# A hybrid decoder layer: gate/up products summed in PSUM, paced weight sums, a new order of the down products

## The chip, the core and the metric

The kernel runs on one core of a Trainium2 chip. The metric is the device time of one execution in microseconds (us). The kernel is compared with an earlier version of itself. An execution is also recorded by the hardware profiler; its times count from the start of the recorded span. TensorE is called PE in the rows, VectorE DVE, ScalarE ACT, GpSimd POOL, and SP is the queue that issues the transfers.

## What is computed

One decoder layer in fp32 with 1024 tokens of width 1024: attention in two kinds, a normalisation, then a feed-forward part (FFN) of width 2816 and a second normalisation. The change is in the FFN:

```
y  = concat(FoX out, GLA out) @ W_o
x  = layer_norm(alpha * x + (1 + gate_m) * y, ln1_g, ln1_b)
u2 = x * (1 + scale_f) + shift_f
h  = silu(u2 @ w_gate) * (u2 @ w_up)          # (1024, 2816)
y2 = h @ w_down                               # (1024, 1024)
x  = layer_norm(alpha * x + (1 + gate_f) * y2, ln2_g, ln2_b)
```

## The kernel before

All operands of matmuls are split in a high part (`hi`, made by an ACT cast, L87) and a low part (`lo`, the rest, made by a DVE subtraction, L88); a product is hi x hi + hi x lo + lo x hi, so three matmuls for each pair of tiles. `split` is that pair of operations.

Gate/up: the 2816 columns are taken in 22 blocks of 128 (index f). In each block, gate and up together form a matrix that is cut in 2 x 2, the input is cut in 2 x 2 as well (A11, A12, A21, A22), and the eight products of the quarters are replaced by seven, P1 to P7, of sums of quarters. The sums of the input (S1 to S4) are made once (`second_operands`), those of the weights (T1 to T4) once a block (`sum_weights`, four DVE operations L982 to L985, and splits). Each product is 12 matmuls of 128 x 512 into a PSUM bank (`product`, L996). P1 and P2 need only A11 and A12, so the first three blocks' P1 and P2 run first, while ACT and DVE make the rest. In `group_parts` P1 and P2 are added up in a half of the two-bank tile `c11`; P3 goes into `y_` on top of P5, P4 (`x_`) on top of P7, P6 has a bank `z_`; DVE and ACT then add the parts: five additions a block on DVE (L1071, L1079, L1081, L1082, L1086) and a multiplication with the gate (L1087).

The down product uses seven products as well. Its sums of h (`h_sums`, stored to DRAM in `a_d`) and of the rows of w_down (`w_sums`, L1034 to L1040, loaded, four DVE operations, stored to `t_d`) are made during gate/up, `w_sums` for two blocks at a time (NI = 11 of them). In `ffn_down` a down product (924 matmuls in all, L1167) is written as `product(banks, columns of a_d, rows of w, new)`; (k, c) names the part k of a_d and the half c of the tokens. It runs over 6 groups: each loads two tiles (`ar`, `raw`), splits them, and multiplies into four banks, `sa` or `sb`. Between products the rows of the residual come in (`rows_in`, L1108 to L1110: a load of z_d, a POOL multiplication with l1g, a POOL addition of l1b), results are added to them (`add_rows`, L1180 on POOL, L1181 on DVE), and `out_norm` (L1231 to L1241) writes the final rows.

The order of the instructions on each engine is set by a scheduler that works from its own estimate of durations, with the program's order as priority; `after(key)` adds the condition that what follows is placed behind a recorded instruction. Pools of fixed slots decide when a tile can be written again: `slot(i)` waits until the last reader of slot i is through.

## Time and profile before

| | us |
|---|---|
| median of 3 runs | 1314.95 |
| lowest, highest | 1314.1, 1317.26 |
| the profiled execution | 1316.09 |
| its span | 1314.4 |
| TensorE busy in the span | 1240.2 |
| DVE busy | 826.6 |
| ACT busy | 507.6 |
| POOL busy | 275.9 |

Busy times overlap, and the share of an engine over the whole span is a mean of stages with different limits. The FFN takes the span from about 609 us on. The page's chain of work that ended last runs for 66% of the span over TensorE, for 13% over transfers and for 10% over DVE. A matmul's record is longer than its distance to the next (0.39 against 0.23 us), since matmuls are pipelined; time is therefore told from start to start.

### The profile page before, as it was taken

Reading aid. Unit: us, or ns where it says so; the run is one execution under the profiler, and the core shown is the slowest. Engines: PE = TensorE matmul, PEld = TensorE weight load, DVE = VectorE, ACT = ScalarE, POOL = GpSimd, SP = SyncE. Lnnn points to the kernel's source line nnn. Section 1 sums busy time; section 2 is a strip of 40 time slices with the busy share of each in tenths; the row PEclk is TensorE's granted clock in tenths of the full one; section 3 lists DMA queues with packets and bytes.
Section 4 is the critical chain, followed back from the end, with each engine's and each line's share of the span. In section 5 each row is a group of like instructions: output and inputs, shape, how many; then the busy total and the mean of one; then the engine's idle time right before and its main releaser. Section 6 shows DMA issues by size and latency. Waiting matters only on the chain.

```text
span 1314.4 us, 16515 instructions
## 1 busy us (share of the span) xinstructions
PE 1240.2 (94%) x6209; PEld 996.8 (76%) x6209; DVE 826.6 (63%) x1207; ACT 507.6 (39%) x858; POOL 275.9 (21%) x264
## 2 busy tenths in 40 slices
PE   6999999999999999999899989999999969999994
PEld 4889987899877656667577768888888847888873
DVE  7656537732465455556987776675675577654768
ACT  3422354523354466565532222332233313443331
POOL 3500023220245355231000000000000067200225
PEclk9999999999999999999999999999999979999988
DMA  9865621112125115144387774332322485666543
GB/s 298 257 224 174 214 65 33 25 25 65 49 97 145 66 33 146 65 144 144 108 259 265 233 253 147 120 113 96 120 70 83 153 325 163 192 208 190 165 142 128
DMA packets 137297, 190.67 MB, mean 145 GB/s; under 512 B 7953, under 2 KB 87931, under 8 KB 137217
## 3 DMA queue, kind: packets, MB, share of 16 engines
q1 hardware_dynamic: 137216, 189.61, 45.2%
q8 instruction: 49, 0.80, 0.3%
...
HBM read 140.94 MB, written 44.32 MB: 141 GB/s over the span
## 4 chain that ended last, share of the span: by engine, by line
PE 66%; DMA 13%; DVE 10%; issue 3%; ACT 3%; POOL 3%; SPq 1%; POOLq 0%; DVEq 0%; ACTq 0%
PE dn L1167 12%; PE gu L996 7%; PE gy L996 6%; PE gx L996 6%; PE pv L791 4%; DMA t_d<-wd 3%; DMA wc<-in_w_c_dram 3%; PE gz L996 3%; DMA wd<-in_w_down_dram 3%; PE tr L781 3%; PE acc L330 3%; PE acc L332 3%; PE acc L331 3%; PE acc L100 2%; PE acc L99 2%
## 5 line engine op out<-in xcount | busy, mean ns | idle before, releaser
L88 DVE TENSOR_TENSOR lo<-raw,hi 128x1024 fp32r<-128x1024 f32 (+1 forms) x112 | 146.4, 1307 | 170.6 <-ACT hi L87 170.5
L87 ACT CAST hi<-raw 128x1024 fp32r<-128x1024 f32 (+1 forms) x112 | 114.8, 1026 | 134.4 <-PE gu L996 46.1
L1167 PE MATMUL dn<-hi,al 128*128 128x512 f32 x280 | 111.1, 402 | 13.6 <-DVE al L88 13.6
L1167 PE MATMUL dn<-lo,ah 128*128 128x512 f32 x280 | 112.4, 401 | 3.5 <-DVE lo L88 3.5
L1109 POOL TENSOR_TENSOR r<-r,l1g 128x1024 f32<-128x1024 f32 x8 | 23.0, 2896 | 437.9 <-PE gu L996 435.5
L1167 PE MATMUL dn<-hi,ah 128*128 128x512 f32 x280 | 110.9, 401 | 1.1 <-ACT ah L87 0.8
L330 PE MATMUL acc<-hi,uh 128*128 128x264 f32 (+1 forms) x384 | 108.8, 284 | 0.9 <-ACT m L531 0.8
L332 PE MATMUL acc<-hi,ul 128*128 128x264 f32 (+1 forms) x384 | 108.7, 284 | 0.0
L331 PE MATMUL acc<-lo,uh 128*128 128x264 f32 (+1 forms) x384 | 108.7, 283 | 0.0
L88 DVE TENSOR_TENSOR al<-ar,ah 128x1024 fp32r<-128x1024 f32 (+1 forms) x38 | 58.2, 1539 | 50.6 <-ACT ah L87 50.5
L1167 PEld LDWEIGHTS dn<-hi,al 128*128 128x128 f32 x280 | 54.0, 193 | 27.7 <-DVE al L88 14.9
L330 PEld LDWEIGHTS acc<-hi,uh 128*128 128x128 f32 x384 | 72.8, 190 | 2.3 <-ACT m L531 1.0
L331 PEld LDWEIGHTS acc<-lo,uh 128*128 128x128 f32 x384 | 72.8, 190 | 0.6 <-issue 0.2
L332 PEld LDWEIGHTS acc<-hi,ul 128*128 128x128 f32 x384 | 72.7, 189 | 0.4 <-issue 0.2
L756 DVE CUSTOM_DVE_ANT_0 pr<-sc,smask 128x128 f32<-128x128 f32 (+7 forms) x64 | 47.6, 754 | 38.1 <-PE sc L752 23.2
L87 ACT CAST ah<-ar 128x1024 fp32r<-128x1024 f32 (+1 forms) x38 | 37.3, 984 | 88.2 <-PE dn L1167 83.4
L1167 PEld LDWEIGHTS dn<-lo,ah 128*128 128x128 f32 x280 | 54.0, 193 | 16.6 <-DVE lo L88 4.3
L996 PE MATMUL gu<-a1h,lo 128*128 128x512 f32 x160 | 63.9, 399 | 2.3 <-DVE lo L88 2.3
L996 PE MATMUL gy<-s,b 128*128 128x512 f32 x264 | 64.5, 391 | 1.1 <-DVE hf L1071 0.6
L1167 PEld LDWEIGHTS dn<-hi,ah 128*128 128x128 f32 x280 | 53.8, 192 | 14.3 <-ACT ah L87 1.2
L786 ACT COPY pt<-tr 128x512 f32<-128x512 f32 x80 | 45.7, 583 | 46.3 <-PE tr L781 39.1
L996 PE MATMUL gu<-a1l,hi 128*128 128x512 f32 x160 | 63.3, 396 | 0.0
...
## 6 DMA issues: line engine op xcount, KB each, us to landing
ar<-a_d SPq DMA_DIRECT2D x35, 512.0 KB, 4.1
wc<-in_w_c_dram SPq DMA_DIRECT2D x32, 512.0 KB, 4.5
raw<-in_w_gate_dram SPq DMA_DIRECT2D x25, 512.0 KB, 5.4
wd<-in_w_down_dram SPq DMA_DIRECT2D x22, 512.0 KB, 4.4
t_d<-wd SPq DMA_DIRECT2D x22, 512.0 KB, 5.2
a_d<-hf SPq DMA_DIRECT2D x22, 512.0 KB, 5.0
u<-in_w_up_dram SPq DMA_DIRECT2D x21, 512.0 KB, 3.9
raw<-t_d SPq DMA_DIRECT2D x20, 512.0 KB
```

The lines of the kernel that those rows point to most:

```text
L87: nc.scalar.copy(dst_hi, src)
L88: return nc.vector.tensor_tensor(dst_lo, src, dst_hi.bitcast(F32), op=ALU.subtract).ins
L99: nc.tensor.matmul(ps, lh, rh, start=start, stop=False)
L330: nc.tensor.matmul(ps, uh[k][:, ts], wh[:, k % 4, :], start=k == 0, stop=False)
L331: nc.tensor.matmul(ps, uh[k][:, ts], wl[:, k % 4, :], start=False, stop=False)
L332: nc.tensor.matmul(ps, ul[k][:, ts], wh[:, k % 4, :], start=False, stop=k == NK - 1)
L756: nc.vector.tensor_tensor_reduce(t[:, 0:nk], sc[:, 0:nk], smask[:, S - nk : S], op0=ALU.add, op1=ALU.min, scale=-1.0, scalar=3e38, accum_o ...
L781: nc.tensor.transpose(tr[:, a * 256 + j * P : a * 256 + (j + 1) * P], ps_[2 * j + par][:, (2 * kk + a) * P : (2 * kk + a + 1) * P], ident,)
L786: nc.scalar.copy(pt[:, par, :], tr)
L791: nc.tensor.matmul(pv[64 * par : 64 * par + 64, 0:256], fv_t(kb)[:, 64 * h : 64 * h + 64], pt[:, par, a * 256 : (a + 1) * 256], start=kb == 0,
L996: nc.tensor.matmul(ps, x, y, start=start and j == 0 and i == 0, stop=j == NJ - 1 and i == 2, skip_group_check=not start,)
L1167: nc.tensor.matmul(ps, x[:, a, qs], y[:, a, :], start=start and a == 0 and i == 0, stop=stop and a == n - 1 and i == 2, skip_group_check=n ...
```

## The change

1. `group_parts`: P6 and P7 and P4 are added in PSUM to P1 in bank `a`, P3 to P5 in `c`; P2 has a bank `b`. DVE adds three times a block (L1077, L1090, L1092), ACT copies three times and applies silu twice. The order is P1 P2 P6 P5 P7 P3 P4; in block 0 P5 comes before P6.
2. `second_operands`: the sums of S3 come first, its splits last but one. P1 and P2 of the first three blocks are written block by block.
3. `w_sums` is called at the blocks WS = 3, 4, 6, 8, 10, 12, 13, 15, 17, 19, 21, each behind that block's load of up weights; `h_sums` of a pair is called in the next pair's first block.
4. `ffn_down`: `sa` is four single banks, `sb` halves of two-bank tiles, the product (3, 0) comes before (2, 1), and the vectors l1g, l1b, gf, l2g, l2b and the residual's rows are loaded between the groups (`between`), behind the loads of the group before. The multiplication with gf goes from POOL to DVE.

```diff
-        stage("S3", 0, a11, a11, a21, ALU.subtract, "t")
-        stage("S1", 1, a21, a21, a22, ALU.add, "sS3")
-        stage("A22", 4, a22, None, None, None, "sS1")
-        stage("S2", 2, a22, a22, a11, ALU.subtract, "lo")
-        stage("S4", 3, a12, a12, a22, ALU.subtract, "sS2")
+        with after("t"):
+            sums(a11, a11, a21, ALU.subtract)
+        stage("S1", 1, a21, "sum", a21, a22, ALU.add)
+        stage("A22", 4, a22, "sum")
+        stage("S2", 2, a22, "lo", a22, a11, ALU.subtract)
+        stage("S3", 0, a11, "sum")
+        stage("S4", 3, a12, "sum", a12, a22, ALU.subtract)
...
-        nc.sync.dma_start(u, w_up[:, f * P : (f + 1) * P].rearrange("(k p) n -> p k n", p=P))
+        last["u"] = nc.sync.dma_start(u, w_up[:, f * P : (f + 1) * P].rearrange("(k p) n -> p k n", p=P)).ins
...
         def p1():
-            product(c11, w["B11"], opnd["A11"], True)
+            if f == 2:
+                st_["a"] = bank("b2", "ga")
+            else:
+                st_["w"] = wide(f"w{par}", "ga")
+                st_["a"] = st_["w"][:, 0:512]
+            product(st_["a"], w["B11"], opnd["A11"], True)
 
...
+            if f < 2:
+                st_["b"] = st_["w"][:, 512:1024]
             else:
...
+                st_["b"] = bank("b3" if f < 4 else f"b{2 + par}", "gb")
+            product(st_["b"], w["B21"], opnd["A12"], True)
...
+        def p6():
+            h = st_["h"] = h_tile(f)
+            nc.scalar.copy(h[:, 0, :], st_["a"])
+            if f == 0:
+                g0 = cp.tile([P, 512], F32, tag="m1", name="g0")
+            else:
+                st_["g"] = slot(HG[par], (2, 512), name="sg")
+                g0 = st_["g"][:, 0, :]
+            st_["g0"] = g0
+            nc.vector.tensor_tensor(g0, st_["b"], h[:, 0, :], op=ALU.add)
+            product(st_["a"], w["T2"], opnd["S2"], False)
+            nc.scalar.activation(g0, g0, AF.Silu)
+            nc.scalar.copy(h[:, 0, :], st_["a"])
+
+        def p5():
+            st_["c"] = bank(f"b{par}", "gc")
+            product(st_["c"], w["T1"], opnd["S1"], True)
+
+        def p73():
+            a, c_, h = st_["a"], st_["c"], st_["h"]
+            nc.scalar.copy(h[:, 1, :], c_)
+            product(a, w["T3"], opnd["S3"], False)
+            nc.vector.tensor_tensor(h[:, 1, :], a, h[:, 1, :], op=ALU.add)
+            product(c_, w["B22"], opnd["S4"], False)
+            nc.vector.tensor_tensor(h[:, 0, :], c_, h[:, 0, :], op=ALU.add)
+
+        def p4():
             h = st_["h"]
...
+            last["p4"] = product(st_["a"], w["T4"], opnd["A22"], False)
+            if f == 0:
+                st_["g"] = slot(HG[par], (2, 512), name="sg")
+            g = st_["g"]
+            nc.scalar.activation(g[:, 1, :], st_["a"], AF.Silu)
...
+            else:
+                nc.vector.tensor_tensor(h, g, h, op=ALU.mult)
...
-        wides = [wide(f"w{1 - i}", "dn") for i in range(2)]
-        sa = [wides[q // 2][:, (q % 2) * 512 : (q % 2 + 1) * 512] for q in range(4)]
-        sb = [bank(f"b{q}", "dn") for q in range(4)]
+        sa = [bank(f"b{q}", "dn") for q in range(4)]
+        wides = [wide(f"w{i}", "dn") for i in range(2)]
+        sb = [wides[q % 2][:, (q // 2) * 512 : (q // 2 + 1) * 512] for q in range(4)]
...
+        def product(banks, asrc, bsrc, new, between={}):
             for m in range(NG):
+                if m in between:
+                    with after("ld"):
+                        between[m]()
                 g = group(m, asrc, bsrc)
...
-            nc.gpsimd.tensor_tensor(t, t, gf[:, hs], op=ALU.mult)
+            gf = cv["gf"]
+            nc.vector.tensor_tensor(t, t, gf[:, hs], op=ALU.mult)
...
-        ra = rows_in(0)
-        product(sa, a_cols(0, 0), w_rows(0, 0), True)
...
+        def gains():
+            cv["l1g"], cv["l1b"] = bcast(14, ln1_g, "l1g"), bcast(15, ln1_b, "l1b")
+            for n in ("l1g", "l1b"):
+                nc.scalar.mul(cv[n], cv[n], ALPHA)
...
+        product(sa, a_cols(0, 0), w_rows(0, 0), True, {2: gains, 3: rows_of(0, 0), 4: rows_of(0, 1), 5: rows_of(0, 2)})
...
+        product(sb, a_cols(1, 0), w_rows(1, 0), True, {1: rows_of(0, 3), 2: load("gf", 22, grow_d[3, :])})
...
+        product(
+            sa, a_cols(2, 0), t_rows(1, 1), False, {3: load("l2g", 24, ln2_g), 5: load("l2b", 26, ln2_b)}
...
+        product(sb, a_cols(0, 1), t_rows(0, 0), True, {m: rows_of(1, m - 1) for m in range(1, 5)})
...
-        rb = rows_in(1)
+        product(sb, a_cols(3, 0), w_rows(1, 1), False)
+        for q in range(4):
+            nc.vector.tensor_tensor(c2[q], sb[q], c2[q], op=ALU.add)
+            add_rows(ra, bsa, q, 1, c2[q])
+            out_norm(0, q, ra[q], bsa[q], l2g, l2b)
         product(sa, a_cols(2, 1), t_rows(0, 1), False)
         bsb = [new_bs() for q in range(4)]
         for q in range(4):
             nc.vector.tensor_tensor(c5[q], sa[q], c5[q], op=ALU.add)
             add_rows(rb, bsb, q, 1, c5[q])
-        product(sb, a_cols(3, 0), w_rows(1, 1), False)
-        for q in range(4):
-            nc.vector.tensor_tensor(c2[q], sb[q], c2[q], op=ALU.add)
-            add_rows(ra, bsa, q, 1, c2[q])
-            out_norm(0, q, ra[q], bsa[q])
...
-        gs[0][0]()
-        gs[1][0]()
-        gs[0][1]()
-        gs[1][1]()
-        gs[2][0]()
-        gs[2][1]()
+        for f in range(3):
+            gs[f][0]()
+            gs[f][1]()
+    WS = [3 + i * 18 // 10 for i in range(NI)]
...
-        p754()
-        p63()
+        if f == 0:
+            p5()
+            p6()
+        else:
+            p6()
+            p5()
         if f >= 2 and f % 2 == 0:
-            w_sums(f // 2 - 1)
-    w_sums(NI - 1)
...
+            h_sums(f // 2 - 1)
+        p73()
+        p4()
+        if f in WS:
+            with after("u"):
+                w_sums(WS.index(f))
+    h_sums(NI - 1)
```

**SP at the second operands.** The rows run from the last store of z_d (its readers are the residual's rows later on) to the first loads for `w_sums`. Before, with `raw` the gate and `u` the up weights of blocks 1 and 2:

```order
L883 DMA z_d<-r_5338 128x1024 [waits Activation_49]
L960 DMA raw_5910<-in_w_gate_dram 128x8x128 [waits DMAHW7_49]
L960 DMA raw_6012<-in_w_gate_dram 128x8x128 [waits DMAHW1_49]
L965 DMA u_6014<-in_w_up_dram 128x8x128 [waits DMAHW0_49,PE_49]
L965 DMA u_5912<-in_w_up_dram 128x8x128 [waits PE_49]
L1034 DMA wd_6105<-in_w_down_dram 128x1024 [waits DMAHW2_49,DVE_49]
L1034 DMA wd_6106<-in_w_down_dram 128x1024 [waits DMAHW3_49,DVE_49]
```

Now:

```order
L883 DMA z_d<-r_5338 128x1024 [waits Activation_49]
L969 DMA u_6000<-in_w_up_dram 128x8x128 [waits PE_49]
L969 DMA u_5909<-in_w_up_dram 128x8x128 [waits DMAHW7_49,PE_49]
L964 DMA raw_5907<-in_w_gate_dram 128x8x128 [waits DMAHW0_49]
L964 DMA raw_5998<-in_w_gate_dram 128x8x128 [waits DMAHW1_49]
L969 DMA u_6118<-in_w_up_dram 128x8x128 [waits DMAHW7_49,DMAHW2_49,DVE_49]
L1039 DMA wd_6220<-in_w_down_dram 128x1024 [waits DMAHW3_49]
L1039 DMA wd_6221<-in_w_down_dram 128x1024 [waits DMAHW4_49,DVE_49]
```

The two up loads, which wait for PE, have moved ahead of the two gate loads.

**DVE at the same place.** `af` and `x` are quarters of the input, L943 (now L942) a sum for S1 to S4, L88 the low part of a split, L982 (now L986) the first sum of a block's weights. Before:

```order
L943 TENSOR_TENSOR af_5340<-af_5340,x_934_5629 128x512 [waits Activation_49]
L943 TENSOR_TENSOR af_5357<-af_5357,x_935_5630 128x512 [waits Activation_49]
L88 TENSOR_TENSOR s_946_5682<-af_5340,s_946_5682 128x512 [waits Activation_49]
L88 TENSOR_TENSOR s_947_5686<-af_5357,s_947_5686 128x512 [waits Activation_49]
L943 TENSOR_TENSOR af_5374<-af_5374,x_936_5631 128x512 [waits Activation_49]
L943 TENSOR_TENSOR af_5391<-af_5391,raw_5632 128x512 [waits Activation_49]
L943 TENSOR_TENSOR x_934_5629<-x_934_5629 128x512
L943 TENSOR_TENSOR x_935_5630<-x_935_5630 128x512
```

Now:

```order
L1077 TENSOR_TENSOR g_5848<-ga_5757,hf_5846 128x512 [waits Activation_49]
L942 TENSOR_TENSOR af_5340<-af_5340,x_934_5629 128x512 [waits Activation_49]
L942 TENSOR_TENSOR af_5357<-af_5357,x_935_5630 128x512 [waits Activation_49]
L942 TENSOR_TENSOR af_5374<-af_5374,x_936_5631 128x512 [waits Activation_49]
L986 TENSOR_TENSOR raw_5907<-u_5909,raw_5907 128x512 [waits DMAHW7_49,DMAHW0_49]
L942 TENSOR_TENSOR af_5391<-af_5391,raw_5632 128x512 [waits Activation_49]
L942 TENSOR_TENSOR x_934_5629<-x_934_5629 128x512 [waits DVE_49]
L942 TENSOR_TENSOR x_935_5630<-x_935_5630 128x512 [waits DVE_49]
L942 TENSOR_TENSOR x_936_5631<-x_936_5631 128x512 [waits DVE_49]
L987 TENSOR_TENSOR u_5909<-u_5909 128x512 [waits DVE_49,PE_49]
```

A weight sum of block 1 that waits for two transfers has moved from behind the splits of S1 to the fifth place, and an addition of block 0's P1 and P2 (L1077) stands ahead.

**PE at the first down product.** `gy` and `gc` are gate/up banks of the last block, `dn` the banks of the down product. Before:

```order
L996 MATMUL gy_8563<-s_962_5742,b_1302_8520 128x512 [waits DVE_49]
L996 MATMUL gy_8563<-s_962_5742,b_1302_8520 128x512 x2
L996 MATMUL gy_8563<-s_963_5746,b_1302_8520 128x512 x3
L996 MATMUL gy_8563<-s_964_5750,b_1302_8520 128x512 x3
L996 MATMUL gy_8563<-s_965_5754,b_1302_8520 128x512 x3
L1167 MATMUL dn_8655<-hi_8683,ah_8681 128x512 [waits Activation_49]
L1167 MATMUL dn_8655<-lo_8684,ah_8681 128x512
L1167 MATMUL dn_8656<-hi_8683,ah_8681 128x512
L1167 MATMUL dn_8656<-lo_8684,ah_8681 128x512
L1167 MATMUL dn_8655<-hi_8683,al_8682 128x512 [waits DVE_49]
```

Now:

```order
L1170 MATMUL dn_8609<-hi_8621,ah_8619 128x512 [waits Activation_49]
L1170 MATMUL dn_8609<-lo_8622,ah_8619 128x512 [waits DVE_49]
L1170 MATMUL dn_8611<-hi_8621,ah_8619 128x512
L1170 MATMUL dn_8611<-lo_8622,ah_8619 128x512
L1170 MATMUL dn_8612<-hi_8621,ah_8619 128x512
L1170 MATMUL dn_8612<-lo_8622,ah_8619 128x512
L1000 MATMUL gc_8534<-s_962_5745,b_1290_8488 128x512 [waits Activation_49]
L1000 MATMUL gc_8534<-s_962_5745,b_1290_8488 128x512 x2
L1000 MATMUL gc_8534<-s_963_5748,b_1290_8488 128x512 x3
L1000 MATMUL gc_8534<-s_964_5751,b_1290_8488 128x512 x3
L1000 MATMUL gc_8534<-s_965_5754,b_1290_8488 128x512 x3
L1170 MATMUL dn_8609<-hi_8621,al_8620 128x512 [waits DVE_49]
```

The first six matmuls of the down product have moved ahead of P3 of the last block; the matmul that needs the low part `al` stands behind it, and P4 of the last block (12 matmuls into `ga`) follows a few rows later.

**DVE at the last two products.** Before, L1223 is the first reading of the last product (1,1), L1238 belongs to `out_norm` of the first half:

```order
L1231 SCALAR_TENSOR_TENSOR r_1330_8673<-r_1330_8673,mv_10018,l2g_8650 128x1024
L1238 SCALAR_TENSOR_TENSOR r_1328_8665<-r_1328_8665,mv_9992,l2b_8652 128x512 [waits DVE_49,Pool_49]
L1238 SCALAR_TENSOR_TENSOR r_1328_8665<-r_1328_8665,mv_9992,l2b_8652 128x512
L1223 TENSOR_TENSOR tmpb<-dn_8655,gf_8648 128x512 [waits PE_49]
L1238 SCALAR_TENSOR_TENSOR r_1329_8669<-r_1329_8669,mv_10005,l2b_8652 128x512 [waits DVE_49,Pool_49]
L1238 SCALAR_TENSOR_TENSOR r_1329_8669<-r_1329_8669,mv_10005,l2b_8652 128x512
L1238 SCALAR_TENSOR_TENSOR r_1330_8673<-r_1330_8673,mv_10018,l2b_8652 128x512 [waits DVE_49,Pool_49]
```

Now, L1244 is the addition of product (2,1), L1271 belongs to `out_norm` of the first half:

```order
L88 TENSOR_TENSOR kp_10070<-ar_10065,kp_10069 128x1024 [waits DMAHW1_49,Activation_49]
L88 TENSOR_TENSOR lo_10000<-raw_9995,hi_9999 128x1024 [waits DMAHW6_49,Activation_49]
L1271 SCALAR_TENSOR_TENSOR r_1358_8879<-r_1358_8879,mv_9760,l2b_9255 128x512 [waits DVE_49,Pool_49]
L1271 SCALAR_TENSOR_TENSOR r_1358_8879<-r_1358_8879,mv_9760,l2b_9255 128x512
L88 TENSOR_TENSOR kp_10072<-raw_10067,kp_10071 128x1024 [waits DMAHW2_49,Activation_49]
L1244 TENSOR_TENSOR dc_9507<-dn_8609,dc_9507 128x512 [waits PE_49]
L88 TENSOR_TENSOR al_10034<-ar_10029,ah_10033 128x1024 [waits DMAHW7_49,Activation_49]
L1244 TENSOR_TENSOR dc_9507<-dn_8610,dc_9507 128x512 [waits PE_49]
```

`out_norm` of the first half stood among the additions of the last product, and now stands ahead of those of the product before it.

## Rows read from the trace of the kernel before

**Rows 1.** Stretch, length, busy (count) PE PEld DVE ACT POOL, clock, DMA, GB/s.

```profile
629.05:655.26 26.21, 20.80 (x73) 13.88 (x72) 26.21 (x44) 14.16 (x23) 0.00 (x0) 0.93 0.40 109
661.00:781.00 120.00, 113.99 (x483) 89.86 (x483) 93.36 (x131) 33.68 (x46) 0.00 (x0) 1.00 0.78 256
781.00:1059.00 278.00, 277.27 (x1198) 225.60 (x1198) 182.36 (x229) 88.60 (x117) 7.99 (x3) 1.00 0.36 122
1059.00:1119.00 60.00, 45.47 (x181) 35.73 (x182) 44.87 (x25) 15.54 (x19) 38.24 (x13) 0.89 0.69 225
1119.00:1260.00 141.00, 141.00 (x611) 114.24 (x610) 80.99 (x82) 56.43 (x66) 16.05 (x8) 1.00 0.61 191
1260.00:1299.00 39.00, 34.38 (x135) 26.93 (x134) 36.43 (x57) 8.46 (x10) 16.22 (x10) 0.91 0.33 114
1299.00:1314.40 15.40, 0.46 (x2) 0.02 (x1) 10.52 (x12) 2.59 (x4) 10.87 (x9) 0.64 0.37 137
```

**Rows 2.** Chain of waits, two neighbouring blocks: start us, length us, what.

```profile
880.65 1.39 PE gu L996 x6
...
900.08 1.39 PE gu L996 x6
```

**Rows 3.** Instructions in order of time, SP's loads from 609 to 655.

```profile
616.34 1.94 SPq L960 DMA_DIRECT2D raw<-in_w_gate_dram  x2
629.01 0.99 SPq L965 DMA_DIRECT2D u<-in_w_up_dram  x2
```

**Rows 4.** DMA issues from 612 to 640: count, size, median us to landing.

```profile
raw<-in_w_gate_dram SPq DMA_DIRECT2D x2, 512.0 KB, 7.0
u<-in_w_up_dram SPq DMA_DIRECT2D x2, 512.0 KB, 5.2
```

**Rows 5.** Instructions in order of time, DVE from 626 to 662: start, length.

```profile
627.48 1.89 DVE L943 TENSOR_TENSOR x<-x 128x512 f32<-128x512 f32 x3
...
636.52 0.68 DVE L982 TENSOR_TENSOR raw<-u,raw 128x512 f32<-128x512 f32 x1
...
649.76 0.68 DVE L88 TENSOR_TENSOR s<-af,s 128x512 fp32r<-128x512 f32 x1
```

**Rows 6.** Waits of DVE from 655 to 782: total us, times, longest.

```profile
DVE wd L1035 <- DMA wd<-in_w_down_dram: 19.4, 9, 4.4
```

**Rows 7.** Instructions in order of time, PE from 1055 to 1115; idle before, releaser.

```profile
1071.98 0.80 PE L1167 MATMUL dn<-hi,al 128*128 128x512 f32 x1 [11.77 <-DVE al L88]
...
1104.02 0.50 PE L1167 MATMUL dn<-hi,al 128*128 128x512 f32 x1 [0.50 <-DVE al L88]
...
1110.71 0.50 PE L1167 MATMUL dn<-lo,ah 128*128 128x512 f32 x1 [0.89 <-DVE lo L88]
...
1113.48 0.50 PE L1167 MATMUL dn<-hi,al 128*128 128x512 f32 x1 [1.35 <-DVE al L88]
```

**Rows 8.** The same view, POOL from 1040 to 1120.

```profile
1059.17 14.99 POOL L1109 TENSOR_TENSOR r<-r,l1g 128x1024 f32<-128x1024 f32 x5 [2.24 <-DVE lo L88]
1092.43 23.25 POOL L1110 TENSOR_TENSOR r<-r,l1b 128x1024 f32<-128x1024 f32 x8 [18.27 <-ACT l1b L1321]
```

**Rows 9.** The same view, DVE from 1052 to 1120 (`gx` lies in PSUM).

```profile
1057.94 1.21 DVE L88 TENSOR_TENSOR lo<-raw,hi 128x1024 fp32r<-128x1024 f32 x1
...
1062.54 3.35 DVE L88 TENSOR_TENSOR lo<-raw,hi 128x1024 fp32r<-128x1024 f32 x1
1065.82 0.68 DVE L1081 TENSOR_TENSOR sg<-gx,hf 128x512 f32<-128x512 f32 x1
```

**Rows 10.** The same view, PE from 1262 to the end.

```profile
1269.97 0.80 PE L1167 MATMUL dn<-lo,ah 128*128 128x512 f32 x1 [2.58 <-DVE lo L88]
...
1289.49 4.40 PE L1167 MATMUL dn<-kp,kp 128*128 128x512 f32 x18 [1.74 <-DVE tmpb L1223]
```

**Rows 11.** The same view, DVE from 1262 to the end.

```profile
1302.55 0.68 DVE L1223 TENSOR_TENSOR tmp<-dn,gf 128x512 f32<-128x512 f32 x1
...
1305.89 2.35 DVE L1231 SCALAR_TENSOR_TENSOR r<-r,mv,l2g 128x1024 f32<-128x1024 f32 x1
```

More of the change, by code (lines that the diff above doesn't have):

```diff
@@ L936, in second_operands, with sums, stage @@
         ops = {n: [] for n in ("A22", "S1", "S2", "S3", "S4")}
[L937 to L945 removed]
         a11, a12 = (lambda j: af[j][:, 0, :]), (lambda j: af[j][:, 1, :])
         a21, a22 = (lambda j: xs[j][:, 0, :]), (lambda j: xs[j][:, 1, :])
[L951 to L955 removed]
+        def sums(out, x, y, op):
+            for j in range(NJ):
+                last["sum"] = nc.vector.tensor_tensor(out(j), x(j), y(j), op=op).ins
+        def stage(name, i, out, key, x=None, y=None, op=None):
+            with after(key):
+                if op is not None:
+                    sums(out, x, y, op)
+                for j in range(NJ):
+                    put(ops, name, S_HL[j][i], out(j))
+        with after("t"):
[5 more added lines that the diff above has]
+        stage("S4", 3, a12, "sum", a12, a22, ALU.subtract)
         opnd.update(ops)
@@ L1144, in group @@
             braw = wtile("raw", (n, 512), F32)
-            nc.sync.dma_start(braw, bsrc(m, n))
+            last["ld"] = nc.sync.dma_start(braw, bsrc(m, n)).ins
             if keep and n == 1:
@@ L1188, in ffn_down @@
             nc.scalar.copy(c1[q], sa[q])
-        product(sb, a_cols(1, 0), w_rows(1, 0), True)
+        product(sb, a_cols(1, 0), w_rows(1, 0), True, {1: rows_of(0, 3), 2: load("gf", 22, grow_d[3, :])})
+        gf = cv["gf"]
+        ra = [cv[(0, q)] for q in range(4)]
         bsa = [new_bs() for q in range(4)]
@@ L1197, in ffn_down @@
             nc.scalar.copy(c2[q], sa[q])
-        product(sb, a_cols(0, 1), t_rows(0, 0), True)
+        product(sb, a_cols(0, 1), t_rows(0, 0), True, {m: rows_of(1, m - 1) for m in range(1, 5)})
+        rb = [cv[(1, q)] for q in range(4)]
         c5 = halves((36, 37))
@@ L1225, in ffn_down, with out_norm @@
             ln_stats(rb[q], 0, bsb[q])
-            out_norm(1, q, rb[q], bsb[q])
-    def out_norm(half, q, r, bs):
+            out_norm(1, q, rb[q], bsb[q], l2g, l2b)
+    def out_norm(half, q, r, bs, l2g, l2b):
         mv = ln_scale(bs)
```

96 lines of the change are left out of this document (26 added, 70 removed).

## The prediction

> **What bounds the kernel now.** Start with the busy time by stretch [rows 1]. From 781 to 1059 us, most of the gate/up blocks, TensorE is busy 277.27 of 278 us at full clock, while DVE is busy 182, ACT 89 and the DMA engines 36%. Nothing there but fewer matmuls would help, and the change keeps their number: 22 blocks x 7 products x 12 = 1848 for gate/up and 924 for down. The chain of waits gives their price: the same place in two neighbouring blocks lies 19.43 us apart for 84 matmuls, 0.2313 us each [rows 2]. With that price any stretch can be read as time lost: its length minus its matmuls x 0.2313. The lost time sits in four places [rows 1]. From 629.05 to 655.26, 73 matmuls (16.9 us) fill 26.2 us: 9.3 lost. From 661 to 781, 483 matmuls fill 120 us: 8.3 lost. From 1059 to 1119, 181 fill 60 us: 18.1 lost. From 1260 to 1299, 135 fill 39 us: 7.8 lost; behind it follow 15.4 us almost without matmuls, the tail. From 1119 to 1260 nothing is lost (611 x 0.2313 = 141.3). The change touches all four and adds no matmul, so it is judged place by place.
>
> **Part 1, the second operands (609 to 655).** After the first three blocks' P1 and P2 (72 matmuls, over at 629.05) TensorE needs the sums S1 to S4 of the input and their splits. DVE makes them without a gap: three 128x512 operations start 0.60 us apart (1.89 us for three), and the last S4 split starts at 649.76 and takes 0.68 [rows 5]. The gate weights of blocks 1 and 2 were issued at 616.34 and the up weights at 629.01 [rows 3]; a pair lands in 7.0 and 5.2 us [rows 4], so the first weight sum came at 636.52 [rows 5] and waited for nothing. The change issues P1 and P2 block by block, so that the slots of block 1's first weights come free after 48 matmuls instead of 72. I put that at 629.05 less 24 matmuls (5.6 us) and less some 2 us of the transposes between them: 622. But on SP the two up loads now stand ahead of the two gate loads, so that all four start at 622 instead of two at 616. Two pairs one after the other, 5.2 to 7.0 us each, bring the first gate weights at about 629 and the last at about 632. On DVE the weight sum that needs them (L986) is now the fifth operation of the stage, ahead of one S3 sum, all S1 sums and every split. So those start at 629.5. From the order, 39 operations of 0.60 and one of 1.15 us then lie up to the last S4 split: it ends near 654.2, where before it ended at 650.4. TensorE loses more than these 4 us. In program order it meets P5, P6 and P3 of block 0 first, and P3 needs S4; P7 and the next block stand behind. So up to 655.2 it does 36 matmuls (8.3 us) in 26.2 us: 17.9 lost against 9.3. With a matmul or two more at the lower clock that such a stop leaves behind, this part costs +9.5. Bounds: if the loads land by 626, DVE ends 3 us earlier: +5. If they land at 635: +15.
>
> **Part 2, w_sums paced, fewer DVE additions.** Before, eleven w_sums run one behind the other from 653 on; DVE waits 19.4 us in 9 waits at L1035 for rows of w_down [rows 6], and the weight splits queue behind those waits: that is the 8.3 us lost from 661 to 781. Now one w_sums goes with about every second block (WS), and its loads are held by a block's up load. At 1.8 blocks or 35 us for each, a load of 512 KB, 5 to 7 us [rows 4], lands long before DVE reaches it. DVE also has two 128x512 additions a block less (-1.2 us of 19.4), and ACT one copy more, 0.76 us at the mean of its operations from 781 to 1059 (88.60/117 [rows 1]); both engines are under 70% busy there, so neither shows. The w_sums now fall into the full blocks: 4 x 0.60 = 2.4 us of DVE every 35 us, covered by the same idle third. I take -8, bounds -8.3 and -3 (a few waits stay).
>
> **Part 3, into the down products (1059 to 1119).** The first group of the first down product waited 11.77 us for its low half `al` (1071.98), and three later waits cost 0.50 + 0.89 + 1.35 = 2.7 [rows 7]; the rest of the 18.1, 3.6 us, is the start itself and the lower clock behind the long wait (0.89 granted over this stretch [rows 1]). Two things lie behind it. SP sends eight row loads and four vectors among the group loads. And POOL multiplies and adds those rows, 3.0 and 2.9 us each [rows 8], beside which a DVE split takes 3.35 instead of 1.21 us [rows 9]. The change takes all rows and vectors out of the start: the loads of the first groups go alone, gains come at group 2, rows one per group from group 3. TensorE also gets 24 gate/up matmuls (P3 and P4 of the last block) between those of group 0. What is left is POOL beside groups 3 to 5 and the start of product 2, the situation of 1092 to 1116, where eight POOL additions cost TensorE 2.7 us in waits [rows 7]. I take 3.5 lost, so -14.5; bounds -18 (none lost) and -3 (the waits only move).
> A row of this stage tells which DVE work suffers: from 1059 to 1074, while POOL worked, the addition that reads PSUM took 0.68 us, as ever, and the split at 1062.54 took 3.35 [rows 8, 9]. The Trainium skill, SBUF — State Buffer, "Who interferes with whom", says that a DVE instruction with two inputs in SBUF shares a port with GpSimd, which holds it for its whole instruction; the trace agrees. By that rule, moving the POOL rows elsewhere saves nothing by itself: the first rival below.
>
> **Part 4, rows of half 1 in product 4.** Eight POOL operations of 2.9 us, 23 us, now stand beside four groups of 5.55 us (24 matmuls). Each group needs two splits: 6.7 us instead of 2.4, so DVE falls behind by about 1 us a group, 4 in all; three buffers for a group's rows (HRAW) let it start two groups ahead, 11 us. Cost 0, bound +4. The gain multiplication of add_rows goes from POOL to DVE: 16 x 0.60 us, in products with DVE at 57% (80.99/141) [rows 1].
>
> **Part 5, the end.** Before, DVE did both halves' last additions and norms together. It began on the last quarter only at 1302.55, some 3 us after the last matmul, and the norm L1231 at 1305.89 took 2.35 us beside POOL [rows 11] where an operation of its size takes 1.21 alone [rows 9]. Now out_norm of half 0 comes a product earlier, so this backlog is gone: the tail is shorter by those 3 us and 1.1 more: -4. In place of the two waits of before (2.58 us at 1269.97, and 1.74 for `tmpb` at 1289.49 [rows 10]) stands a new one. Products (2,1) and (1,1) both go into `sa`, so TensorE waits at their border for the four additions L1244, which stand on DVE behind out_norm(0). DVE has some 34 us to do in the 30.5 us of product (2,1): 16 operations of 0.60 for the rows of half 0, four norms of 1.2 and eight halves of 0.65, a dozen splits of 1.2 for the groups, and 1 us of small ones. So it is 3.5 us late, and with about 3 more at the lower clock this stands against the 7.8 of before: -1. Together -5, bounds -9 and +2.
>
> **Rivals.** (a) *POOL and DVE collide as before, only later.* There are still 16 POOL operations of 2.9 us, and beside each a split is 2.1 us longer. Against it: DVE now meets them with a lead, and from 1092 to 1116 eight of them cost only 2.7 us. If the first product pays like the mults of before, 11 of the 14.5 us stay: 1308. (b) *Part 1 costs nothing and part 3 loses nothing*: the four loads land before DVE is there. 1297 - 9.5 - 3.5 = 1284. Against it: two pairs took 7.0 and 5.2 us. (c) *Slower: the banks come free too late.* P6 and P7, and P4, now add into bank `a`, which ACT copies or DVE reads between two of them, with one product (2.78 us) as cover each time; P3 does so in `c`. DVE queues splits (1.2 us) and w_sums before those reads. A wait of 1.2 us in each of 19 full blocks gives +23: 1320. It turns the sign from 1.0 us a block on. For it: four such borders a block where before there were three (c11, x_, y_), and DVE reads are the longest queue. Against it: with those three TensorE lost 0.7 us in these 278 us, and DVE has a third of its time free [rows 1]. (d) *The pacing does not hold*, loads or DVE still meet the w_sums in a bunch: part 2 gives nothing, 1305.
>
> **How the numbers follow.** 1314.4 (span) + 9.5 - 8 - 14.5 + 0 - 5 = 1296.4. The profiled run, 1316.09, lay 1.7 above its span, and the median 1314.95 1.1 below the profiled run: **1297**. Chances: forecast 0.48, (a) 0.18, (b) 0.13, (c) 0.12, (d) 0.09. A difference under 0.3% (1311 to 1319) is what a measurement of this kernel can't tell from none. A third of (a), 0.06, and a sixth of (c), 0.02, fall there: same 0.08. Slower is the rest of (c), 0.10. Faster: 0.82. The range from 1284 to 1312 leaves out (c), a sixth of (a) and a third of (b), 0.19; its ends are also what the bounds of parts 1 and 3 give from the forecast (-13, +15).
>
> **What would show it.** Part 1: S4's last split near 654 and about 36 matmuls from 629 to 655; P1/P2's end at 629. Part 2: no waits over 1 us from 670 to 1050, 19.4 us a block. Part 3: no wait over 3 us at the first L1170 matmuls, and the full clock there. Part 5: a wait of about 3 us at the start of product (1,1), the last matmul 10 to 11 us before the end. I am wrong if blocks take over 20 us each (c), or if DVE splits beside POOL stop TensorE for over 5 us (a).

## The result

| | before | changed |
|---|---|---|
| time, median (lowest to highest) | 1314.78 (1314.1 to 1317.26) | 1293.18 (1290.69 to 1297.26) |
| profiled execution / its span | 1316.09 / 1314.4 | 1297.26 / 1295.2 |
| ratio, 95% interval | | 0.9835 [0.9807, 0.9864] |

The change is faster by 1.65%: 21.6 us between the medians, 19.2 between the spans. The forecast was 1297 in a range of 1284 to 1312. A second timing of the changed kernel gave 1297.39 (1293.27 to 1297.81), ratio 0.9866 [0.9837, 0.9895], with a span of 1295.7 in its profiled execution. The two profiled spans lie within 0.5 us, but the spans of all eight executions run from 1288.6 to 1295.7, and the median moves by 4 us from one timing to the next. Small differences between kernels are therefore read stage by stage from the traces below, one for each kernel.

**The same stretches in the kernel after** (busy time by stretch, columns as in [rows 1]):

```profile
629.05:655.26 26.21, 17.61 (x57) 12.23 (x57) 25.82 (x42) 11.87 (x20) 0.00 (x0) 0.86 0.22 65
...
670.00:781.00 111.00, 111.00 (x482) 90.46 (x481) 72.46 (x95) 36.95 (x52) 0.00 (x0) 1.00 0.46 163
781.00:1052.00 271.00, 270.60 (x1170) 219.78 (x1168) 169.97 (x220) 91.45 (x126) 0.00 (x0) 1.00 0.45 158
...
1060.00:1120.00 60.00, 56.41 (x243) 45.29 (x243) 39.43 (x25) 22.62 (x27) 22.73 (x8) 1.00 0.73 248
1120.00:1245.00 125.00, 124.52 (x538) 100.70 (x537) 89.97 (x96) 50.33 (x58) 29.94 (x12) 1.00 0.65 213
1245.00:1284.00 39.00, 35.47 (x143) 28.35 (x142) 34.97 (x50) 10.01 (x12) 8.57 (x6) 0.91 0.33 115
```

From 670 to 781 TensorE now never stops, where 8.3 us were lost before (from 661 to 781); from 1060 to 1120 it loses 3.8 us (60 less 243 x 0.2313) instead of 18.1. The first stretch went the other way: 57 matmuls where before there were 73.

**Time lost, by matmul.** Both kernels issue the same 2772 matmuls of gate/up and down, and the trace holds them all. Take the start of the n-th, subtract the start of the first and (n-1) x 0.2313 us [rows 2], and what is left is the time lost up to there. Differences of that count give one column for each stage, in us. The tail is the span's end less the last matmul's start. The first column is the start of matmul 1, which no edit here aims at; it differs by up to 3.7 us from kernel to kernel, so "rest" (span less that start) is the number to compare.

| kernel | first | operands (to 201) | w_sums (to 651) | blocks (to 1701) | transition (to 2051) | products (to 2561) | end | tail | span | rest |
|---|---|---|---|---|---|---|---|---|---|---|
| before | 609.0 | 12.9 | 8.6 | 0.1 | 19.2 | 0.2 | 8.2 | 15.3 | 1314.4 | 705.4 |
| changed | 609.4 | 22.7 | -0.1 | 0.6 | 4.2 | 0.9 | 6.4 | 10.2 | 1295.2 | 685.8 |
| changed, again | 610.2 | 23.6 | -0.1 | 0.5 | 4.2 | 0.9 | 5.3 | 10.2 | 1295.7 | 685.5 |
| e1_wsums_bunched | 608.2 | 21.9 | 7.5 | -0.5 | 3.5 | 0.9 | 5.3 | 10.2 | 1297.9 | 689.7 |
| e2_rows_start | 608.9 | 22.2 | -0.1 | 0.5 | 13.5 | -0.3 | 6.5 | 10.2 | 1302.4 | 693.5 |
| e3_loads_start | 607.4 | 22.3 | -0.1 | 0.0 | 13.6 | -0.3 | 6.4 | 10.2 | 1300.6 | 693.2 |
| e4_before_no_pool | 607.7 | 12.9 | 8.2 | 0.1 | 5.1 | 0.2 | 9.3 | 13.8 | 1298.2 | 690.5 |
| e5_sums_late | 608.4 | 17.7 | 0.1 | -0.2 | 4.2 | 2.7 | 5.3 | 10.2 | 1289.4 | 681.0 |
| e6_norm_late | 608.4 | 22.6 | -0.1 | 0.0 | 1.8 | 0.9 | -0.2 | 21.1 | 1295.5 | 687.1 |
| e7_order_back | 608.7 | 23.7 | -0.1 | 0.0 | 1.3 | 2.0 | 0.0 | 21.2 | 1297.7 | 689.0 |
| e9_copies_late | 606.5 | 17.3 | 0.1 | 0.1 | 4.2 | 0.8 | 5.2 | 10.2 | 1285.3 | 678.8 |
| e10_norm_split | 609.2 | 16.8 | 0.1 | -0.2 | 4.2 | 2.6 | -0.2 | 16.3 | 1289.9 | 680.7 |
| e11_no_pool_half0 | 609.2 | 22.6 | -0.1 | 0.0 | 0.1 | 0.9 | 5.3 | 10.2 | 1289.2 | 680.0 |

The change by this table: start +0.4, operands +9.8, w_sums -8.7, blocks +0.5, transition -15.0, products +0.7, end -1.8, tail -5.1: -19.2, the difference of the spans.

**The second operands, after.** Instructions in order of time (start, length, what was idle before), SP and then DVE; and TensorE's waits from 605 to 700 us (total, times, longest):

```profile
622.05 1.01 SPq L969 DMA_DIRECT2D u<-in_w_up_dram  x2
623.10 2.63 SPq L964 DMA_DIRECT2D raw<-in_w_gate_dram  x2
...
629.44 0.69 DVE L986 TENSOR_TENSOR raw<-u,raw 128x512 f32<-128x512 f32 x1 [3.38 <-DMA raw<-in_w_gate_dram]
...
652.26 2.50 DVE L88 TENSOR_TENSOR s<-af,s 128x512 fp32r<-128x512 f32 x4
```

```profile
PE ga L1000 <- DVE s L88: 6.7, 2, 5.3
PE ga L1000 <- ACT raw L899: 3.8, 1, 3.8
PE gc L1000 <- DVE s L88: 1.9, 2, 1.7
```

The up loads stand ahead of the gate loads [rows 3], the first weight sum waits 3.38 us for the gate weights where before it waited for nothing [rows 5], and the last split of S4 ends at 654.76. The three rows are five waits and 12.4 us; the longest, 5.3, is for a split of S. The 3.8 us is a stop that the prediction did not have.

**The transition, after.** TensorE's waits from 1060 to 1120, then POOL and DVE in order of time (answers to [rows 7 to 9]):

```profile
PE dn L1170 <- DVE lo L88: 3.6, 2, 2.0
```

```profile
1061.56 8.09 POOL L1203 TENSOR_TENSOR r<-r,l1g 128x1024 f32<-128x1024 f32 x3 [447.82 <-DMA r<-z_d]
1077.96 9.08 POOL L1204 TENSOR_TENSOR r<-r,l1b 128x1024 f32<-128x1024 f32 x3 [8.31 <-ACT l1b L1196]
...
1064.09 3.32 DVE L88 TENSOR_TENSOR lo<-raw,hi 128x1024 fp32r<-128x1024 f32 x1 [4.29 <-ACT hi L87]
1070.66 1.21 DVE L88 TENSOR_TENSOR al<-ar,ah 128x1024 fp32r<-128x1024 f32 x1
1081.39 6.20 DVE L88 TENSOR_TENSOR lo<-raw,hi 128x1024 fp32r<-128x1024 f32 x2
```

POOL still does the rows of half 0 here, and a split that meets it takes 2.7 to 3.4 us instead of 1.21. TensorE waits 3.6 us for them in two stops, where before it waited 14.5 (11.77 and 2.7 [rows 7]).

**The end, after.** TensorE's waits from 1240 on, and DVE in order of time:

```profile
PE dn L1170 <- DVE dc L1244: 3.5, 1, 3.5
```

```profile
1251.16 0.68 DVE L1244 TENSOR_TENSOR dc<-dn,dc 128x512 f32<-128x512 f32 x1
...
1285.46 0.69 DVE L1256 TENSOR_TENSOR tmp<-dn,gf 128x512 f32<-128x512 f32 x1
```

The new stop at the border of products (2,1) and (1,1) is there at the forecast size. DVE takes up the last quarter at 1285.46, at once behind the last matmul (1285.0); before it came some 3 us late [rows 11].

### The profile page after: what moved, and what is told of

Read it like the earlier page. It is cut to its first block, busy times and chain, and to the rows that moved or that the text cites. A ratio compares the mean times of both kernels' runs of the same rounds, so it can differ in the third digit from the quotient of the medians.

```text
span 1295.2 us, 16488 instructions
## 1 busy us (share of the span) xinstructions
PE 1233.6 (95%) x6209; PEld 995.4 (77%) x6209; DVE 800.4 (62%) x1176; ACT 520.6 (40%) x880; POOL 254.4 (20%) x252
## 4 chain that ended last, share of the span: by engine, by line
PE 74%; DMA 9%; DVE 8%; ACT 3%; issue 3%; POOL 2%; SPq 1%; POOLq 0%; DVEq 0%; ACTq 0%
PE ga L1000 18%; PE dn L1170 14%; PE gc L1000 8%; DMA wc<-in_w_c_dram 5%; PE gb L1000 4%; PE pv L791 4%; PE tr L781 3%; PE acc L330 2%; PE acc L332 2%; PE acc L331 2%; PE acc L100 2%; PE acc L99 2%; PE acc L101 2%; PE sc L751 1%; PE sc L752 1%
## 5 line engine op out<-in xcount | busy, mean ns | idle before, releaser
L88 DVE TENSOR_TENSOR lo<-raw,hi 128x1024 fp32r<-128x1024 f32 (+1 forms) x112 | 148.2, 1324 | 105.5 <-ACT hi L87 97.7
L1203 POOL TENSOR_TENSOR r<-r,l1g 128x1024 f32<-128x1024 f32 x8 | 23.5, 2949 | 499.1 <-DMA r<-z_d 499.1
L1000 PE MATMUL ga<-s,hi 128*128 128x512 f32 x352 | 111.8, 397 | 6.8 <-DVE s L88 6.7
L88 DVE TENSOR_TENSOR al<-ar,ah 128x1024 fp32r<-128x1024 f32 (+1 forms) x38 | 54.6, 1439 | 51.5 <-ACT ah L87 51.5
L1000 PEld LDWEIGHTS ga<-s,hi 128*128 128x128 f32 x352 | 67.0, 190 | 23.8 <-DVE s L88 7.8
L1000 PE MATMUL ga<-s,lo 128*128 128x512 f32 x176 | 70.3, 400 | 0.0
L1000 PE MATMUL gc<-s,b 128*128 128x512 f32 x264 | 64.3, 392 | 0.0
```

The lines of the kernel that those rows point to most:

```text
L88: return nc.vector.tensor_tensor(dst_lo, src, dst_hi.bitcast(F32), op=ALU.subtract).ins
L1000: ins = nc.tensor.matmul(ps, x, y, start=start and j == 0 and i == 0, stop=j == NJ - 1 and i == 2, skip_group_check=not start,)
```

## The experiments

### Part 2: the pacing of w_sums

```diff
-        if f in WS:
-            with after("u"):
-                w_sums(WS.index(f))
+        if f >= 2 and f % 2 == 0:
+            w_sums(f // 2 - 1)
...
+    w_sums(NI - 1)
```

> The changed kernel, with w_sums called again as in the kernel before: one behind every second block from block 2 on, not held by a block's load of up weights. Theory (the crowding of the eleven w_sums cost the 8 us from 661 to 781): about 7 us longer than the changed kernel, near 1300, with waits of DVE for rows of w_down of 15 us or more between 655 and 785 and some 7 us of TensorE time lost there. Rival (the two DVE additions fewer a block made the room, pacing adds nothing): within 2 us of the changed kernel, and no waits of TensorE over 1 us between 670 and 785.

Measured: 1300.45 us (1299.74 to 1303.51), ratio to the kernel before 0.9901 [0.9885, 0.9917]. The column of the w_sums loses 7.5 us again. TensorE and DVE in order of time:

```profile
721.12 0.60 PE L1000 MATMUL gc<-s,lo 128*128 128x512 f32 x1 [1.88 <-DVE lo L88]
...
717.78 0.69 DVE L1041 TENSOR_TENSOR wd<-wd,wd 128x512 f32<-128x512 f32 x1 [1.85 <-DMA wd<-in_w_down_dram]
...
758.12 0.69 DVE L1041 TENSOR_TENSOR wd<-wd,wd 128x512 f32<-128x512 f32 x1 [3.96 <-DMA wd<-in_w_down_dram]
```

DVE stands up to 4 us at a weight sum for its rows, and TensorE waits at 721 for a split that is queued behind such a stand (717.78). So 7.5 of the 8.7 us are the pacing, not the new block order or the fewer additions. The rest rises by 4 us only, since it lost 3.7 us less in other columns (0.8 in the operands, 1.1 in the blocks, 0.7 in the transition, 1.1 at the end), which the edit does not explain.

### Part 3: what the long wait was

> The kernel before, with POOL's multiplication and addition on the residual's eight rows left out (so the rows enter the result without their gain and offset); the loads stay where they are. If POOL beside DVE made the wait of 11.8 us at the first down product: the splits there take 1.2 us instead of 2.8 to 3.4, the wait shrinks to under 4 us, and the kernel is 10 to 14 us shorter than before, 1301 to 1305. If the row loads in front of the group loads made it: the wait stays above 9 us and the kernel gains at most 4 us (the later three waits of 2.7 us).

```diff
-            nc.gpsimd.tensor_tensor(r, r, l1g, op=ALU.mult)
-            nc.gpsimd.tensor_tensor(r, r, l1b, op=ALU.add)
```

Measured: 1300.31 us (1298.47 to 1301.15), ratio 0.9893 [0.9867, 0.992]. This is the kernel *before* with its old order and all its row loads at the start. TensorE's waits from 1050 to 1125, and one of DVE's splits:

```profile
PE dn L1165 <- DVE al L88: 2.5, 1, 2.5
PE dn L1165 <- ACT ah L87: 0.7, 1, 0.7
```

```profile
1059.65 1.22 DVE L88 TENSOR_TENSOR al<-ar,ah 128x1024 fp32r<-128x1024 f32 x1
```

The wait of 11.77 [rows 7] is 2.5, every split takes 1.2 us, and the stage loses 5.1 instead of 19.2. POOL beside DVE costs these 14 us. The 5 that are left stand with the loads at the start and the old order, which this run does not part.

> The changed kernel, with the vectors and the residual's eight rows loaded and worked on by POOL at the start of the down products, as in the kernel before. Theory (the 18 us of before came from both, row loads among the group loads and POOL's work beside DVE's splits): 8 to 14 us longer than the changed kernel, 1301 to 1307, with waits of TensorE of 8 us or more in the first 60 us of the down products. Rival (the gain came from the 24 gate/up matmuls that now stand between those of the first group, and from the order of its loads): within 3 us of the changed kernel.

```diff
+        gains()
+        for h in range(2):
+            for q in range(4):
+                rows_of(h, q)()
+        load("gf", 22, grow_d[3, :])()
...
-        product(sa, a_cols(0, 0), w_rows(0, 0), True, {2: gains, 3: rows_of(0, 0), 4: rows_of(0, 1), 5: rows_of(0, 2)})
+        product(sa, a_cols(0, 0), w_rows(0, 0), True)
...
```

Measured: 1303.89 us (1300.09 to 1307.74), ratio 0.9922 [0.9895, 0.9948]. The changed kernel with all rows and vectors at the start loses 13.5 us in the transition, 9.3 more. POOL in order of time, and TensorE's waits:

```profile
1056.79 16.64 POOL L1203 TENSOR_TENSOR r<-r,l1g 128x1024 f32<-128x1024 f32 x6 [443.52 <-PE gc L1000]
1073.60 5.92 POOL L1203 TENSOR_TENSOR r<-r,l1g 128x1024 f32<-128x1024 f32 x2 [0.18 <-DMA r<-z_d]
1079.48 25.57 POOL L1204 TENSOR_TENSOR r<-r,l1b 128x1024 f32<-128x1024 f32 x8
```

```profile
PE dn L1170 <- DVE al L88: 5.5, 2, 4.1
PE dn L1170 <- DVE lo L88: 3.5, 2, 2.2
```

POOL works 48 us almost without a gap, and four matmul groups wait for their splits. So the spreading of the rows and vectors, not the new place of P3 and P4, carries the greater part of the gain: 9.3 of the 15 us return when it alone is undone. The other 5.7 stay; no run parts the place of P3 and P4 from the order of the group loads.

> As the run with rows and vectors at the start, but only the transfers stand there; POOL multiplies and adds the rows where the changed kernel does. If POOL beside DVE is what cost the time: within 2 us of the changed kernel. If the transfers among the group loads cost it: as long as the run with both at the start. If half and half: in the middle, 4 to 7 us above the changed kernel.

```diff
+            for q in range(4):
+                row_in(h, q)
...
-                nc.sync.dma_start(r, z_d[t * P : (t + 1) * P, :])
...
+        product(sa, a_cols(0, 0), w_rows(0, 0), True, {3: rows_of(0, 0), 4: rows_of(0, 1), 5: rows_of(0, 2)})
...
```

Measured: 1302.88 us (1302.14 to 1304.56), ratio 0.9918 [0.9886, 0.9949]. This was to move the transfers alone, but POOL began at 1054.96 as in the run above: a row that has landed lets POOL go, since the order held only what stands on the issuing engine. The run is a second copy of e2_rows_start and doesn't part transfers from arithmetic. e4_before_no_pool and the next run do.

> The changed kernel without the two POOL operations (times l1g, plus l1b) on each of the four rows of half 0; the rows are still loaded, so this leaves out that arithmetic. Theory: the two stops left in the transition (1084.84 and 1094.96, 3.6 us together, both for the low half of a split on DVE) come from DVE splits of 3.3 instead of 1.2 us beside these POOL operations; without them the stops go and 1060 to 1120 loses nothing: 1289 to 1290 us against 1293.2. Rival: the stops come from the rows of w_down and the down operands landing late, or from ACT's casts ahead; they stay, and the time is 1292 to 1294.

```diff
-                nc.gpsimd.tensor_tensor(r, r, cv["l1g"], op=ALU.mult)
-                nc.gpsimd.tensor_tensor(r, r, cv["l1b"], op=ALU.add)
+                if half:
+                    nc.gpsimd.tensor_tensor(r, r, cv["l1g"], op=ALU.mult)
+                    nc.gpsimd.tensor_tensor(r, r, cv["l1b"], op=ALU.add)
```

Measured: 1289.68 us (1288.21 to 1292.41), ratio 0.9808 [0.9786, 0.983]. Busy time by stretch:

```profile
1055.00:1120.00 65.00, 65.00 (x283) 52.79 (x282) 29.28 (x30) 26.19 (x31) 0.00 (x0) 1.00 0.78 268
```

With the same loads (DMA engines 78% busy), TensorE is busy 65.00 of 65 us: the theory holds, and the last 4.2 us of the transition are POOL too. What these eight operations cost is not fixed, though. In e6_norm_late and e7_order_back (below), whose edits come later in the kernel, the same operations cost 1.8 and 1.3 us. There `l1b` is ready earlier and POOL's additions begin some 3 us sooner, counted from the first matmul. POOL and TensorE's waits from 1045 to 1125 in e7_order_back:

```profile
1074.36 9.42 POOL L1204 TENSOR_TENSOR r<-r,l1b 128x1024 f32<-128x1024 f32 x3 [3.68 <-ACT l1b L1196]
```

```profile
PE dn L1170 <- DVE lo L88: 1.0, 1, 1.0
```

### Part 1: which work on DVE delays the sums

```diff
-            sum_weights(f, g, load_up(f), w)
+            u = load_up(f)
+            with after("sum") if f < 3 else nullcontext():
+                sum_weights(f, g, u, w)
```

> The changed kernel, with the weight sums of blocks 1 and 2 placed behind the sums for S1 to S4, so that nothing of S1 to S4 waits for a transfer of weights. Theory (the stage from 629 to 655 is set by DVE's list up to the last S4 split, and 3.4 us of it are a wait for gate weights, and some five weight operations of 0.6 us stand in it): the last S4 split ends near 650 instead of 654.8, TensorE loses 4 to 5 us less, about 1289. Rival (what is late next are the weights of block 1, which now come behind S4): the same time within 1.5 us, with the waits moved behind 655.

Measured: 1287.6 us (1283.62 to 1291.13), ratio 0.9798 [0.9773, 0.9822]. The operands lose 17.7 us instead of 22.7. DVE in order of time:

```profile
644.24 1.29 DVE L986 TENSOR_TENSOR raw<-u,raw 128x512 f32<-128x512 f32 x2
...
646.04 2.49 DVE L88 TENSOR_TENSOR s<-af,s 128x512 fp32r<-128x512 f32 x4
```

The weight sums now stand behind the S sums, and the splits of S4 end at 648.53. Counted from the first matmul that is 5.3 us earlier than in the changed kernel (40.1 against 45.4 us), and TensorE gets 5.0 of them back. The step of the prediction, weight sums that wait for a late load and stand ahead of the sums and splits of S on DVE, is shown by removing it; how much of the 5.3 us was the wait (3.38) and how much the weight operations themselves, this run does not part. The products column rises to 2.7: in product 4 two splits beside POOL now stop TensorE; in the changed kernel none of them does.

> The version with the late weight sums, and in it the copies of product P1 of blocks 0 and 1 on ACT stand behind the last scaled copy of the transposes (L899 of the changed kernel), with the table load and the activation of block 0 behind them. Theory: in the changed kernel the matmuls of block 2 waited 3.76 us for that last L899, since ACT had other work between the eight of them; with the copy away it comes 0.5 to 2 us earlier, the stop shrinks by as much and the lower clock behind it with it: 1285 to 1286 us against 1287.6 without this edit. Rival: the sums and splits on DVE set the end of this stage, the stop at the first S matmuls grows by what this one shrinks, and the time stays at 1287 to 1288.

```diff
...
-            nc.scalar.copy(h[:, 0, :], st_["a"])
+            with after("x2") if f < 2 else nullcontext():
+                nc.scalar.copy(h[:, 0, :], st_["a"])
...
```

Measured: 1287.75 us (1287.04 to 1290.48), ratio 0.9795 [0.9774, 0.9815]. TensorE in order of time, its two stops behind ACT:

```profile
624.40 0.79 PE L1002 MATMUL ga<-a1h,hi 128*128 128x512 f32 x1 [3.27 <-ACT raw L899]
...
639.01 0.50 PE L1002 MATMUL gc<-s,b 128*128 128x512 f32 x1 [2.33 <-ACT s L87]
```

The first stop shrinks by 0.5 us and the operands lose 17.3, against 17.7 in e5_sums_late and 16.8 in e10_norm_split, which has the same code in this stage. That is no gain: the time is that of e5_sums_late, as the rival has it. Of the 4.1 us by which the span is shorter, 1.9 are this run's earlier first matmul (606.5) and 1.9 the products column (0.8 against 2.7), which the edit does not aim at. With so small a change of the first stop, the run doesn't show what the whole stop is worth. What would shorten it stays open: four casts still stand among the eight scaled copies on ACT, and they were not moved.

### Part 5: the new stop at the end

```diff
-            out_norm(0, q, ra[q], bsa[q], l2g, l2b)
...
-            nc.vector.tensor_tensor(c5[q], sa[q], c5[q], op=ALU.add)
-            add_rows(rb, bsb, q, 1, c5[q])
+            last["c5"] = nc.vector.tensor_tensor(c5[q], sa[q], c5[q], op=ALU.add).ins
+        with after("c5"):
+            for q in range(4):
+                out_norm(0, q, ra[q], bsa[q], l2g, l2b)
+                add_rows(rb, bsb, q, 1, c5[q])
```

> The changed kernel, with out_norm of the first half placed behind the four additions that read the banks of product (2,1), so that the last product finds its banks free. Theory (the wait of 3.5 us at the start of the last product and the lower clock behind it, 6.9 us together, are DVE's backlog of out_norm): the wait goes to under 0.5 us, and since DVE then has some 10 us more beside the last product, up to 3 come back in the tail: 1287 to 1290. Rival (DVE has as much to do before the end either way): the wait goes but the tail grows by the same, 1293 within 1.5 us.

Measured: 1299.05 us (1296.96 to 1301.75), ratio 0.9887 [0.9867, 0.9907]. The end column falls from 6.4 to -0.2: the stop is gone, so it did come from `out_norm` ahead of L1244. But the tail grows from 10.2 to 21.1. POOL and DVE in order of time:

```profile
1280.47 5.67 POOL L1271 TENSOR_TENSOR r<-r,l2b 128x512 f32<-128x512 f32 x3
...
1288.42 3.41 DVE L1273 SCALAR_TENSOR_TENSOR r<-r,mv,l2b 128x512 f32<-128x512 f32 x2 [3.40 <-POOL mv L831]
```

The last norm on DVE waits 3.40 us for POOL, which computes its scale (L831) behind 5.67 us of additions of `l2b`, released late by DVE's own backlog. End and tail are one queue of DVE and POOL work.

> The changed kernel, with the down products in the order of the kernel before, (2,1) ahead of (3,0), all else as changed. Theory (the tail became 5.4 us shorter because out_norm of the first half is done before the last product): the tail is again 14 to 15 us instead of 10, the wait for the banks at the last product's start is gone, together 1 to 4 us longer than the changed kernel: 1294 to 1297. Rival (the tail was shortened by the gain multiplication that left POOL, and by the single banks): tail near 10 us and no wait at the start of the last product, so 4 to 7 us shorter, 1286 to 1289.

```diff
+        product(sa, a_cols(2, 1), t_rows(0, 1), False)
+        bsb = [new_bs() for q in range(4)]
...
         product(sb, a_cols(3, 0), w_rows(1, 1), False)
...
-        product(sa, a_cols(2, 1), t_rows(0, 1), False)
...
```

Measured: 1298.74 us (1297.44 to 1300.16), ratio 0.9881 [0.9864, 0.9898]. With (2,1) ahead of (3,0) again no product waits (end 0.0), the last matmul starts 8 us earlier than in the changed kernel, counted from the first, and the tail is 21.2 us: the direction was right, the tail is larger than I wrote. Relative to the changed kernel, the order of the products is worth about 4.6 us over end and tail (21.2 against 16.6). Before, the two were 23.5 together with the same order as here; no run parts the 2.3 us between.

> The version with the late weight sums, and in it two of the four norms of half 0 (q = 2 and 3) stand behind the additions L1244 instead of ahead of them. Theory: the stop of 3.5 us at the border of products (2,1) and (1,1) is two norms long, so it goes; behind the last matmul DVE has room for two norms but not for four (all four made a tail of 20.7 us), so 2 to 4 us are won: 1284 to 1286 against 1287.6. Rival: from product (2,1) on DVE works without a gap, so whatever leaves the stop comes back in the tail: matmuls end 5 us earlier, the tail is 15 us instead of 10, the time stays at 1287 to 1288.

```diff
-            out_norm(0, q, ra[q], bsa[q], l2g, l2b)
+            if q < 2:
+                out_norm(0, q, ra[q], bsa[q], l2g, l2b)
...
+        with after("c5"):
+            for q in range(2, 4):
+                out_norm(0, q, ra[q], bsa[q], l2g, l2b)
...
```

Measured: 1290.2 us (1288.85 to 1291.62), ratio 0.9806 [0.9785, 0.9828]. The stop is gone here too, and the tail is 16.3 us: end and tail together 16.1, against 15.5 in e5_sums_late. DVE in order of time:

```profile
1283.12 2.42 DVE L1276 SCALAR_TENSOR_TENSOR r<-r,mv,l2b 128x512 f32<-128x512 f32 x2 [2.18 <-POOL mv L831]
```

The rival holds: what leaves the stop comes back in the tail, with the same wait for POOL. To win here, work has to leave DVE and POOL, not move among them. Of all versions run, e5_sums_late is the one to keep; its two descendants gave nothing beyond it.

## Why the prediction was right, point by point

- **Sum.** Forecast of the span 1296.4, measured 1295.2. The median of 1293.18 lies 4 below its own profiled execution (1297.26), the highest of its four runs; I had taken 1.1. The second timing (1297.39) doesn't have that gap, so it is scatter and no step. Two sums of the prediction are off without touching the forecast: the bounds of parts 1 and 3 give -8 and +17 from the forecast, not -13 and +15 (the -13 is that of rival (b)), and the terms of DVE's work in part 5 add up to 35 us, not 34, unless the two splits of the sixth group, half the size, are taken at 0.7 us.
- **Part 1: +9.5, measured +9.8.** The loads at 622, the first weight sum at 629.5 and the end of S4 near 654.2 came at 622.05, 629.44 and 654.76. One step was wrong: "P1/P2's end at 629". Block 2's P1 waits 3.76 us for the last scaled copy of the transposes on ACT, with the lower clock behind it, and P1 and P2 end near 636 (matmul 73 starts at 635.9, against 629.0 before). So 6.4 of the 9.8 us are lost before matmul 73, where I had nothing, and only 3.3 behind it. The total held because the end of the splits on DVE sets it: matmul 108, the last of P3 of block 0, starts at 655.44, 0.7 us behind the last split of S4, and the forecast had 72 + 36 = 108 matmuls done by 655.2. From 629 to 655 it did 57 matmuls, where I had 36, since 21 of the first 72 were still to do. e5_sums_late shows the mechanism; what the early stop is worth by itself no run shows.
- **Part 2: -8, measured -8.7.** e1_wsums_bunched gives 7.5 of it back. One step was too strong: the rows of w_down do not land "long before DVE reaches" them. From 655 to 785 DVE still waits 8.5 us for them in six waits (before, 26.3 in 17), but TensorE no longer stops for it.
- **Part 3: -14.5, measured -15.0**, with 3.5 us forecast to be left and 3.8 to 4.2 left. e4_before_no_pool and e11_no_pool_half0 show the cause, e2_rows_start that the spreading is what removed it. Rival (a) would have needed 11 us more and did not come. My reason, that DVE meets POOL with a lead, is half of it: in e2_rows_start the low halves of groups 1 and 2 are ready 12 and 16 us ahead of their use, just as in the changed kernel, and sixteen POOL operations in one run use that up. The low half of group 3 ends there at 1080.60, as TensorE waits for it, and the stage loses 13.5. That in the changed kernel the lead holds because the sixteen come in two batches of eight fits these rows, but was not varied by itself. The rule of the Trainium skill that I weighed there (SBUF — State Buffer, "Who interferes with whom") agrees with the lengths of the splits, 1.2 us alone and 2.7 to 3.4 beside POOL; it doesn't tell what the long splits cost TensorE, which was 14 us in the order of before and 1.3 to 4.2 in the new one. That by this rule moving the rows saves nothing by itself was too strict: undoing it alone costs 9.3 us.
- **Part 4: 0, measured +0.7** (0.9 in the products column, 0.2 before). The longer splits beside POOL from 1143.93 to 1168.9 were covered: TensorE waits for none of them, and its one wait there, 0.5 us at 1187.11, is for an ACT copy (L1235). The cover is thin: in e5_sums_late, e7_order_back and e10_norm_split two of these splits cost 1.5 us together.
- **Part 5: -5, measured -6.9.** The stop of 3.5 us stands where I put it and at that size. End: -1 forecast, -1.8 measured. Tail: -4 forecast, -5.1 measured, since DVE was not late at all.
- **Rival (c), the slower case**: from 700 to 1050 TensorE waits once, 0.4 us, and that for a split of weights (DVE lo L88), not for a bank. The reads of the banks always came within the product between. **(d)**: no stop over 1 us from 670 to 1050.
- What I could not have read from the trace of before: the stop behind ACT (part 1), and that end and tail trade one for one (e6, e7, e10).
